# A streaming-encoder block on one core: weight sums of the second feed-forward made ahead and kept in DRAM, and more products by the seven-product form

## The chip, the core and the metric

The kernel runs on one core of one Trainium2 chip, in one launch. The metric is the time of an execution in microseconds (us); less is better. Engines are named as in the profile: PE (TensorE) multiplies matrices, DVE (VectorE) and ACT (ScalarE) work elementwise, POOL (GpSimd) here only issues some transfers and fills, SP (SyncE) issues nearly all transfers.

## What is computed

One layer over 256 tokens of 2048 features, in float32, cut to what matters here:

```python
def swiglu(h, w_up, w_down):
    gate, up = jnp.split(h @ w_up, 2, axis=-1)
    return (jax.nn.silu(gate) * up) @ w_down

x = x + 0.5 * swiglu(rms_norm(x, ffn1_norm), ffn1_w_up, ffn1_w_down)     # w_up 2048 x 11264, w_down 5632 x 2048
x = x + (sigmoid(gate_A) * hgrn2(h) + sigmoid(gate_B) * rglru(h)) @ w_out  # h = rms_norm(x) @ w_in, projected
x = x + cross_attention(rms_norm(x), rms_norm(mem))                       # 4 heads, 256 memory tokens
x = x + 0.5 * swiglu(rms_norm(x, ffn2_norm), ffn2_w_up, ffn2_w_down)
return rms_norm(x, final_norm)
```

The two feed-forwards are of one form. All that lies between them (projections, recurrences, branch merge, cross attention) is called the middle here.

## The kernel before

**Precision.** Each float32 operand is split into a high part `h` (rounded to the fp32r format by an ACT copy) and a low part `l = raw - h` (by DVE), as `split` does (L119 to L121). A product is then three matmuls: high by high, low operand by high weight, high operand by low weight (`three`, L448 to L454).

**Weights** come in pieces of 1 MB (128 partitions x 2048 float32), one after another in the order of `plan`. `weights()` (L165 to L182) hands a piece out and has the next one prepared ahead; `prepare` (L195 to L221) issues the load on SP's queue into `raw` (three buffers) and splits it into `h` (pool of three) and `l` (pool of three). A piece of kind "added" goes another way (`begin_added`, L186 to L193): a load into `own`, an ACT copy with scale -1 into `l`, and an accumulating transfer on POOL's queue that adds `own` to it, so that DVE has no part in it.

**A feed-forward** (`ffn`, from L467) walks 11 groups of 512 hidden columns. A group has eight up pieces; a piece p holds the four 128x512 blocks (two feature blocks, gate and up) of one pair of feature blocks. Then come two or four down pieces of earlier groups. The activation of a group goes through `ev`, is turned by transposes into `hidop`, and is used by the down pieces later. An up piece is multiplied in one of three forms (table `PRODUCTS`, L460 to L466), each product being three matmuls of 512 columns:

- "plain" (group 0): eight products;
- "mixed": eight products, with differences of the operand;
- "fast": seven products (24 matmuls become 21) out of sums and differences of the four operand blocks and of the four weight blocks, in the manner of Strassen and Winograd.

For a "fast" piece the sums of the weights are made each time: three DVE instructions (L213 to L215) write `td`, four blocks of 512 columns; `td` is then split into `th` (from the `h` pool) and `tl` in two halves. `td` and `tl` both come from the pool "wide", which has three buffers; `ev` and a scratch tile come from it too.

Before the change, both feed-forwards have the same list (`ffn_order`): groups 1 and 2 have four mixed and four fast pieces, groups 3 to 10 have two mixed (0 and 6) and six fast ones. The mixed ones from group 3, piece 6, on are "added".

**The order of the work.** The first pieces are ordered by hand; after that the order of instructions on each engine and on SP's queue is set when the program is built, and doesn't change while it runs. Matmuls of neighbouring pieces may stand interleaved. An engine and a queue work through their list in order, and an instruction whose operand or buffer isn't free holds up those behind it.

Of the kernel before, what the change touches and what calls it, by code (L numbers as in the profile page):

```python
# [13 lines left out]
P = 128  # L14
# [24 lines left out]
PAD = 16  # L39


def ffn_order():

    out, down = [("plain", 0, p) for p in range(8)], [("down", 0, 1, c, 0) for c in range(4)]
    for g in range(1, NG):
        if g < 3:  # L50
            out += [(("mixed", "fast")[p % 2], g, p) for p in (0, 1, 2, 3, 5, 4, 7, 6)]
# [10 lines left out]
def block_kernel(ctx: ExitStack, tc: tile.TileContext, xT, xin, memT, vec, gfin, bgate, lruw, wu1, wd1, win, wv,  # L62
# [55 lines left out]

    def split(h, l, raw):  # L119
        done["high"] = act.activation(h, raw, ACT.Copy).ins  # L120
        dve.tensor_tensor(out=l, in0=raw, in1=h.bitcast(F32), op=ALU.subtract)  # L121
# [6 lines left out]
    orders = dict.fromkeys(("ffn1", "ffn2"), ffn_order())  # L128

    def plan_ffn(name, wu, wd):  # L130
        for e in orders[name]:
            src = wd[e[4], e[3]] if e[0] == "down" else wu[e[1], e[2]]
            kind = "fast" if e[0] == "fast" else "added" if e[0] == "mixed" and e[1:] > (3, 0) else "plain"
            plan.append(((name,) + e, src, kind))

    def plan_columns(name, w, which):
# [3 lines left out]
        plan.extend(((name, g, kq), w[g, kq], "plain") for kq in range(w.shape[1]))  # L140

    plan_ffn("ffn1", wu1, wd1)
    for hf in range(2):
# [21 lines left out]
    def weights(*key):  # L165
        while plan and len(ahead) < 2:
            i = next(planned)
            k, src, kind = plan.pop(0)
            if i == 0:
                in_turn.enter_context(tc.manual_schedule(engines={sp.engine, act.engine, dve.engine}))  # L170
            if i < len(head):
                head[i]()
            if plan and plan[0][2] == "added":
                begun.append(begin_added(plan[0][1]))
            ahead.append((k, prepare(src, kind, 4 if i < 4 else 1)))
            if i in rest:
# [5 lines left out]
        return w  # L182

    begun = []

# [9 lines left out]
    def prepare(src, kind, cuts=1):  # L195
# [8 lines left out]
        if kind == "plain":  # L204
            h, l = split_tiles()
            for a in range(0, 2048, n):
                sp.dma_start(raw[:, a:a + n], src[:, a:a + n])
                split(h[:, a:a + n], l[:, a:a + n], raw[:, a:a + n])
            return h, l
        sp.dma_start(raw, src)  # L210
        td = scoped["wide"].tile([P, 2048], F32, name="td", tag="wide")
        two = [v[:, a:a + 1024].rearrange("p (i n) -> p i n", i=2) for v, a in ((td, 0), (raw, 512))]
        dve.tensor_tensor(out=two[0], in0=raw[:, None, :512].broadcast_to([P, 2, 512]), in1=two[1], op=ALU.subtract)  # L213
        dve.tensor_tensor(out=td[:, 1024:1536], in0=raw[:, 1024:1536], in1=td[:, :512], op=ALU.subtract)
# [122 lines left out]
            return r  # L337


    FFN_POOLS = dict(wide=3, own=1)  # L340

    class TokenSquares:

# [4 lines left out]
        def add(self, c, ts=range(2)):  # L348
            for t in ts:
                if "wide" in scoped:  # L350
                    junk = scoped["wide"].tile([P, 2048], F32, name="junk", tag="wide")[:, :512]
                else:
                    junk = scoped["tmp2"].tile([P, 512], F32, name="junk", tag="tmp2")
# [48 lines left out]

    BOTH = [2, 4]
    xd = []

    def operand_pairs(src, gain, q, xg, out):

        for a in src:  # L410
            i = len(out)
            g = xg[:, i * 512:(i + 1) * 512]
            for z in range(2):
                act.activation(g[:, z * T:][:, :T], a[:, z * T:(z + 1) * T], ACT.Copy,
                               scale=col(gain, 4 * q + 2 * i + z))
            h, l = slot(F32R, "xh"), slot(F32R, "xl")
            split(h[:, :512], l[:, :512], g)
            less = None if i else (h[:, 512:768], l[:, 512:768])
            if 2 * q + i in BOTH:
                if 2 * q + i == BOTH[0]:  # L420
                    xd.append(slot(F32R, "xd"))
                n = 512 * BOTH.index(2 * q + i)
                less = [xd[-1][:, a:a + 256] for a in (n, n + 256)]
            out.append(((h, l), less))

        def sums(which=((0, "less"), (0, "sums"), (1, "less"), (1, "sums"))):
            s = slot(name="xs")
            for i, ((h, l), less) in enumerate(out):
                a = [xg[:, i * 512 + j * P:][:, :P] for j in range(4)]

                def made(h, l, n, at, terms):
# [2 lines left out]
                        dve.tensor_tensor(out=o[j], in0=x, in1=y, op=op)  # L434
                    split(h, l, s[:, at:at + n * P])

                if less and (i, "less") in which:
                    made(*less, 2, 0, lambda o: ((a[0], a[1], ALU.subtract), (a[2], a[3], ALU.subtract)))
                if (i or 2 * q in BOTH) and (i, "sums") in which:
                    if not i and len(which) > 1:  # L440
# [26 lines left out]
    def ffn(name, pairs, sq, then, begin=(), sums=(), rstds=()):  # L467
# [39 lines left out]
        for at, e in enumerate(order):  # L507
# [3 lines left out]
            if kind != "down":  # L511
# [65 lines left out]
    def head_x(p):  # L577
# [7 lines left out]
        sums = operand_pairs([src[:, a:a + 512]], "ffn1_norm", q, xg, out)  # L585
        if p % 2:
            sums1.append(sums)
        pairs1.append(out[-1])
# [466 lines left out]

    def to_ffn(c):
        out = []
        sums2.append(operand_pairs(turned(xt[c]), "ffn2_norm", c, slot(name="xg"), out))
        pairs2.extend(out)
        if c < 2:  # L1060
            sums2.pop(0)()
# [130 lines left out]
```

## Time and profile before

| what | value |
|---|---|
| median of 3 runs | 2442.7 us (2442.57 to 2443.22) |
| the profiled execution's own time | 2442.24 us |
| its span, first to last instruction | 2440.5 us |
| PE, DVE, ACT busy, share of the span | 100%, 78%, 57% |
| HBM read, written | 472.07 MB, 2.10 MB |
| weights of the middle, first and last issue | 677.1 and 1709.4 us from the span's start |

Busy time is summed over an engine's instructions; matmuls overlap, so a matmul's own duration is longer than its share of the time. The granted clock (PEclk) is the share of full speed that TensorE was given. A DMA issue is counted from the issuing instruction to the landing of the last byte. In a row of a group of instructions stand: line, engine, operation, what is written and read, shapes and count; busy us and mean ns of one; and idle time of the engine before them, with what ended it.

### The profile page before, as it was taken

What the parts mean: (1) busy time and instruction counts of PE and PEld (TensorE: products, weight loads), DVE (VectorE), ACT (ScalarE), POOL (GpSimd) and SP (SyncE); (2) the same over time, 40 slices, a digit from 0 to 9 for tenths busy, and PEclk for the clock granted to TensorE, in tenths of its full rate; (3) what the DMA queues carried; (4) which work ended last, traced back from release to release, by engine and by line L of the source; (5) the groups of instructions that cost most, each with busy time, mean ns of one, the idle gap of its engine ahead of it and who ended that gap; (6) DMA issues with size and microseconds to landing.
All of it is one profiled execution on the core that took longest, in us unless ns stands there. A gap on an engine that the chain in (4) does not pass through costs nothing.

```text
span 2440.5 us, 30183 instructions
## 1 busy us (share of the span) xinstructions
PE 2430.0 (100%) x12250; PEld 2033.8 (83%) x12250; DVE 1892.8 (78%) x2016; ACT 1390.8 (57%) x1398; POOL 28.3 (1%) x36
## 2 busy tenths in 40 slices
PE   9999999999999999999999999999999999999998
PEld 8888888888888888888888888888888888888887
DVE  6999999999765757577565676556589999999995
ACT  8566666666554454477435554555555666666664
POOL 0000000000000000000000000000000000000000
PEclk9999999999999999999999999999999999999999
DMA  8557777677555545445555555544555677777763
GB/s 296 207 204 243 255 234 236 234 241 239 200 181 192 180 173 179 176 171 217 191 189 186 206 196 190 190 173 155 189 191 185 232 238 234 234 239 241 237 216 151
DMA packets 75020, 507.59 MB, mean 208 GB/s; under 512 B 8320, under 2 KB 8576, under 8 KB 15232
## 3 DMA queue, kind: packets, MB, share of 16 engines
q1 hardware_dynamic: 69840, 473.06, 53.3%
q0 software_dynamic: 4320, 31.46, 6.7%
q8 instruction: 96, 1.57, 0.2%
q10 hardware_dynamic: 720, 1.13, 0.1%
q14 instruction: 44, 0.36, 0.0%
HBM read 472.07 MB, written 2.10 MB: 194 GB/s over the span
## 4 chain that ended last, share of the span: by engine, by line
PE 97%; DVE 1%; ACT 1%; DMA 1%; issue 0%; SPq 0%; ACTq 0%; DVEq 0%
PE acc L451 18%; PE acc L454 18%; PE acc L452 18%; PE acc L231 11%; PE acc L252 8%; PE acc L253 8%; PE acc L255 8%; PE acc L235 6%; PE acc L491 1%; PE acc L391 1%; ACT h L120 0%; PE acc L768 0%; DVE l L121 0%; DMA xf<-xT 0%; PE acc L1051 0%; PE acc L1006 0%
## 5 line engine op out<-in xcount | busy, mean ns | idle before, releaser
L121 DVE TENSOR_TENSOR l<-raw,h 128x2048 fp32r<-128x2048 f32 (+2 forms) x422 | 877.9, 2087 | 364.8 <-ACT h L120 354.7
L120 ACT ACTIVATE h<-raw 128x2048 fp32r<-128x2048 f32 (+2 forms) x422 | 736.7, 1752 | 615.1 <-PE acc L253 206.2
L451 PE MATMUL acc<-h,xh 128*128 128x512 f32 x1280 | 499.0, 391 | 0.4 <-ACT h L120 0.3
L452 PE MATMUL acc<-h,xl 128*128 128x512 f32 x1280 | 496.9, 389 | 0.0
L120 ACT ACTIVATE h<-td 128x1024 fp32r<-128x1024 f32 x224 | 229.7, 1056 | 177.0 <-PE acc L452 130.8
L252 PE MATMUL acc<-h,ops 128*128 128x512 f32 x832 | 326.9, 393 | 0.0
L253 PE MATMUL acc<-h,ops 128*128 128x512 f32 x832 | 324.3, 390 | 0.0
L121 DVE TENSOR_TENSOR tl<-td,h 128x1024 fp32r<-128x1024 f32 x224 | 267.4, 1220 | 31.6 <-ACT h L120 29.0
L451 PEld LDWEIGHTS acc<-h,xh 128*128 128x128 f32 x1280 | 240.3, 188 | 53.2 <-ACT h L120 3.4
L452 PEld LDWEIGHTS acc<-h,xl 128*128 128x128 f32 x1280 | 240.3, 188 | 49.4
L231 PE MATMUL acc<-ops,h 128*128 128x512 f32 x1152 | 277.9, 393 | 0.2
L451 PE MATMUL acc<-h,hidop 128*128 128x512 f32 x704 | 275.7, 392 | 0.0
L452 PE MATMUL acc<-h,hidop 128*128 128x512 f32 x704 | 274.3, 390 | 0.0
L231 PEld LDWEIGHTS acc<-ops,h 128*128 128x128 f32 x1152 | 211.9, 188 | 42.8 <-DVE ops L292 0.9
L454 PE MATMUL acc<-l,xh 128*128 128x512 f32 x832 | 218.3, 389 | 0.0
L255 PE MATMUL acc<-l,ops 128*128 128x512 f32 x832 | 206.1, 390 | 0.0
L454 PE MATMUL acc<-l,hidop 128*128 128x512 f32 x704 | 188.3, 389 | 0.0
L255 PEld LDWEIGHTS acc<-l,ops 128*128 128x128 f32 x832 | 156.2, 188 | 32.4
L454 PEld LDWEIGHTS acc<-l,xh 128*128 128x128 f32 x832 | 156.0, 188 | 32.5
L252 PEld LDWEIGHTS acc<-h,ops 128*128 128x128 f32 x832 | 156.3, 188 | 32.3
L253 PEld LDWEIGHTS acc<-h,ops 128*128 128x128 f32 x832 | 156.3, 188 | 31.6
L454 PEld LDWEIGHTS acc<-l,hidop 128*128 128x128 f32 x704 | 132.2, 188 | 27.5
(220 smaller groups left out, 2347.9 us busy)
## 6 DMA issues: line engine op xcount, KB each, us to landing
raw<-wu SPq DMA_DIRECT2D x142, 1024.0 KB, 4.8
raw<-wd SPq DMA_DIRECT2D x88, 1024.0 KB, 4.8
raw<-win SPq DMA_DIRECT2D x40, 1024.0 KB, 4.8
raw<-wg SPq DMA_DIRECT2D x32, 1024.0 KB, 4.8
own<-wu SPq DMA_DIRECT2D x30, 1024.0 KB, 5.4
l<-own POOLq DMA_DIRECT2D x30, 1024.0 KB, 7.7
raw<-wab SPq DMA_DIRECT2D x16, 1024.0 KB, 4.8
raw<-wout SPq DMA_DIRECT2D x16, 1024.0 KB, 4.8
```

Of the source, the lines that this page charges most:

```text
L120: done["high"] = act.activation(h, raw, ACT.Copy).ins
L121: dve.tensor_tensor(out=l, in0=raw, in1=h.bitcast(F32), op=ALU.subtract)
L231: pe.matmul(acc, h[:, k * P:(k + 1) * P], xs[k], start=k == 0, stop=False)
L235: done["product"] = pe.matmul(acc[:, :T], l[:, k * P:(k + 1) * P], xs[k][:, :T], start=False, stop=k == KT - 1).ins
L252: pe.matmul(accs[t], x[:, t * P:][:, :P], h[j], start=first and j == 0, stop=False)
L253: pe.matmul(accs[t], x[:, T + t * P:][:, :P], h[j], start=False, stop=False)
L255: done["product"] = pe.matmul(accs[t], x[:, t * P:][:, :P], l[j], start=False, stop=last and j == 3).ins
L391: pe.transpose(accs[m // 2][:, m % 2 * T + t * P:][:, :P], tile[:, t * 512 + m * P:][:, :P], ident)
L451: pe.matmul(acc, ah, bh, start=start, stop=False)
L452: pe.matmul(acc, al, bh, start=False, stop=False)
L454: pe.matmul(acc, ah, bl, start=False, stop=stop)
L491: pe.transpose(acc[:, z * T + t * P:][:, :P], hid[t][:, (2 * y + z) * P:][:, :P], ident)
```

## The change

- **More fast pieces.** In the first feed-forward groups 3 to 10 have one mixed piece (6) in place of two. In the second, groups 1 and 2 have two mixed pieces (4 and 6) in place of four, and groups 3 to 10 have none. The order within groups 3 to 10 becomes 1, 3, 0, 6, 4, 2, 5, 7.
- **Sums made ahead.** For 52 of the second feed-forward's up pieces (list `MADE`: six in groups 1 and 2; pieces 0, 3, 4, 5 and 7 in groups 3 to 10) the sums of the weights are made during the middle: POOL's queue loads the piece into one buffer `made`, DVE makes four subtractions in place, POOL's queue stores the result to a tensor in DRAM. The 52 are spread over 170 pieces of the middle, and the subtractions stand two pieces behind their load.
- **Their use.** A made piece loads three quarters of its weights into `raw` and its sums, 1 MB, into `td`, both on SP's queue; `td` is split in one go.
- **Down pieces of the first feed-forward**: half of those of groups 1 to 8 become "added".
- **Buffers and operands.** The middle's pool `tmp` has six buffers in place of eight, `feature` two in place of three; a pool "third" is added for the feed-forwards. Which operand pairs get sums and which get differences follows from the new lists; three late sums of the first feed-forward are made at pieces 22, 23 and 24 in place of two at 17 and 18.

```diff
+MIXED = {
+    "ffn1": {1: (0, 2, 4, 6), 3: (6,)},
+    "ffn2": {1: (4, 6), 3: ()},
+}
+MADE = [(g, p) for g in range(1, NG) for p in range(8) if p not in ((4, 6) if g < 3 else (1, 6, 2))]
...
-            out += [("mixed" if p in (0, 6) else "fast", g, p) for p in (1, 3, 0, 4, 2, 6, 5, 7)]
+            out += [("mixed" if p in mixed[3] else "fast", g, p) for p in (1, 3, 0, 6, 4, 2, 5, 7)]
...
+    dram = pool("dram", 1, space=bass.MemoryType.DRAM)
...
-            kind = "fast" if e[0] == "fast" else "added" if e[0] == "mixed" and e[1:] > (3, 0) else "plain"
+            kind = "fast" if e[0] == "fast" else "plain"
+            if e[0] == "mixed" and e[1] > 2:
+                kind = "added"
+            if name == "ffn2" and e[0] == "fast" and e[1:] in MADE:
+                src, kind = (src, e[1:]), "made"
+            if name == "ffn1" and e[0] == "down" and 0 < e[1] < NG - 2 and (e[3] + e[4] - e[1]) % 2 == 0:
+                kind = "added"
...
+    between = between + 2, len(plan) - between - 6
...
+            make_ahead(i - between[0])
...
+    def make_ahead(i):
+
+        n, pieces = len(MADE), between[1]
+        if 0 <= i < pieces:
+            for j in range(i * n // pieces, (i + 1) * n // pieces):
+                makers.append((i + 2, make_sums(*MADE[j])))
+        while makers and (makers[0][0] == i or i == pieces):
+            makers.pop(0)[1]()
+
+    def make_sums(g, p):
+        raw = scoped["made"].tile([P, 2048], F32, name="made", tag="made")
+        r = [raw[:, i * 512:(i + 1) * 512] for i in range(4)]
+        nc.gpsimd.dma_start(raw, wu2[g, p])
+
+        def sums():
+            with tc.issue_after(done["low"]):
+                for o, a, b in ((1, 0, 1), (0, 0, 2), (2, 2, 1), (3, 3, 2)):
+                    dve.tensor_tensor(out=r[o], in0=r[a], in1=r[b], op=ALU.subtract)
+            kept = sums_kept[g, p] = dram.tile([P, 2048], F32, name=f"kept{g}_{p}", tag=f"kept{g}_{p}")
+            nc.gpsimd.dma_start(kept, raw)
+
+        return sums
...
+        td = scoped["wide"].tile([P, 2048], F32, name="td", tag="wide")
+        if kind == "made":
+            sp.dma_start(raw[:, 512:], src[0][:, 512:])
+            sp.dma_start(td, sums_kept[src[1]])
+            h, l = split_tiles()
+            split(h[:, 512:], l[:, 512:], raw[:, 512:])
+            th = hp.tile([P, 2048], F32R, name="h", tag="h")
+            tl = scoped["wide"].tile([P, 2048], F32R, name="tl", tag="wide")
+            split(th, tl, td)
+            return (h, l), (th, tl)
         sp.dma_start(raw, src)
-        td = scoped["wide"].tile([P, 2048], F32, name="td", tag="wide")
...
-    FFN_POOLS = dict(wide=3, own=1)
+    FFN_POOLS = dict(wide=3, own=1, third=1)
...
+                    if b in (4, 5) and fast and name == "ffn2" and (g, p) in MADE:
+                        b = 9 - b
...
-    for q, i in ((1, 17), (2, 18)):
+    for q, i in ((0, 22), (1, 23), (2, 24)):
         rest[i] = lambda q=q: sums1[q](((0, "sums"),))
...
-    middle.enter_context(scope(tmp=8, tmp2=2, scores=1, extra=2, feature=3))
+    middle.enter_context(scope(tmp=6, tmp2=2, scores=1, extra=2, feature=2, made=1))
```

More of the change, by code (lines that the diff above doesn't have):

```diff
@@ L50, in ffn_order @@
         if g < 3:
-            out += [(("mixed", "fast")[p % 2], g, p) for p in (0, 1, 2, 3, 5, 4, 7, 6)]
+            out += [("mixed" if p in mixed[1] else "fast", g, p) for p in (0, 1, 2, 3, 5, 4, 7, 6)]
         else:
-            out += [("mixed" if p in (0, 6) else "fast", g, p) for p in (1, 3, 0, 4, 2, 6, 5, 7)]
+            out += [("mixed" if p in mixed[3] else "fast", g, p) for p in (1, 3, 0, 6, 4, 2, 5, 7)]
         if g > 2 and g % 2:
@@ L142, in block_kernel @@
     plan_ffn("ffn1", wu1, wd1)
+    between = len(plan)
     for hf in range(2):
@@ L398, in normed, with operand_pairs @@
             ops.add(accs[m // 2][:, m % 2 * T:][:, :T], col(gain, 4 * c + m))
-    BOTH = [2, 4]
     xd = []
-    def operand_pairs(src, gain, q, xg, out):
+    def operand_pairs(name, src, gain, q, xg, out):
+        mixed = MIXED[name]
+        both = [p for p in mixed[1] if p not in mixed[3]]
         for a in src:
@@ L417, in operand_pairs @@
             split(h[:, :512], l[:, :512], g)
-            less = None if i else (h[:, 512:768], l[:, 512:768])
-            if 2 * q + i in BOTH:
-                if 2 * q + i == BOTH[0]:
+            less = None if 2 * q + i not in mixed[1] else (h[:, 512:768], l[:, 512:768])
+            if 2 * q + i in both:
+                if 2 * q + i == both[0]:
                     xd.append(slot(F32R, "xd"))
-                n = 512 * BOTH.index(2 * q + i)
-                less = [xd[-1][:, a:a + 256] for a in (n, n + 256)]
+                n = 512 * both.index(2 * q + i)
+                less = [xd[-1][:, a:a + 256] for a in (n, n + 256)] if n < 1024 else []
             out.append(((h, l), less))
@@ L435, in made @@
                     split(h, l, s[:, at:at + n * P])
+                if less == [] and (i, "less") in which:
+                    third = scoped["third"].tile([P, 512], F32R, name="xd", tag="xd")
+                    less.extend((third[:, :256], third[:, 256:]))
                 if less and (i, "less") in which:
                     made(*less, 2, 0, lambda o: ((a[0], a[1], ALU.subtract), (a[2], a[3], ALU.subtract)))
-                if (i or 2 * q in BOTH) and (i, "sums") in which:
-                    if not i and len(which) > 1:
+                if 2 * q + i not in mixed[3] and (i, "sums") in which:
+                    if not i and less and len(which) > 1:
                         s = slot(name="xs")
@@ L1057, in to_ffn @@
         out = []
[L1058 removed]
+        sums2.append(operand_pairs("ffn2", turned(xt[c]), "ffn2_norm", c, slot(name="xg"), out))
         pairs2.extend(out)
```

12 lines of the change are left out of this document (7 added, 5 removed).

## The prediction, made before the changed kernel had run

> **What bounds the kernel now.** First the page, then the busy time by stretches. Rows of the first fence: busy time of TensorE; granted clock; chain that ended last, by engine.
>
> ```profile
> PE 2430.0 (100%) x12250; PEld 2033.8 (83%) x12250; DVE 1892.8 (78%) x2016; ACT 1390.8 (57%) x1398; POOL 28.3 (1%) x36
> ...
> PEclk9999999999999999999999999999999999999999
> ...
> PE 97%; DVE 1%; ACT 1%; DMA 1%; issue 0%; SPq 0%; ACTq 0%; DVEq 0%
> ```
>
> TensorE is never out of work: a matmul less is time less, so long as its operands are there. The stretches (start:end, length, then busy us and instructions of PE, PEld, DVE, ACT, POOL, clock, DMA share, GB/s) are the middle with its seams and one group of the second feed-forward:
>
> ```profile
> 651.00:1790.00 1139.00, 1138.76 (x6474) 965.52 (x6473) 721.03 (x856) 598.34 (x701) 1.91 (x2) 1.00 0.52 184
> ...
> 1949.00:2011.00 62.00, 62.00 (x280) 51.40 (x279) 57.26 (x56) 38.34 (x32) 1.72 (x2) 1.00 0.73 238
> ```
>
> In the group DVE has 4.7 us to spare of 62, the DMA engines a quarter; the middle has slack in both. The pace, from the timeline of TensorE, where two "fast" pieces begin (21 matmuls each):
>
> ```profile
> 2082.35 0.39 PE L451 MATMUL acc<-h,xh 128*128 128x512 f32 x1
> ...
> 2087.11 0.39 PE L451 MATMUL acc<-h,xh 128*128 128x512 f32 x1
> ```
>
> 4.76 us for 21 matmuls is 0.227 us each; one ends 0.16 us after its slot, as it lasts 0.39.
>
> **What the change takes away.** Eight "mixed" pieces of the first feed-forward and 20 of the second become "fast": 28 products of three matmuls, 84 x 0.227 = **19.0 us**, 5.4 in the first and 13.6 in the second. TensorE's list in the changed program is indeed 84 matmuls shorter. If nothing ran late, 2442.7 - 19 = 2424.
>
> **What it puts on the path: second feed-forward.** The prices (first instructions grouped by form, the two ACT rows below; then DMA issues with the median us to landing; then, of a stretch with three loads 2.2 us apart, the issues and the landings):
>
> ```profile
> L121 DVE TENSOR_TENSOR l<-raw,h 128x2048 fp32r<-128x2048 f32 x294 | 671.4, 2289 | 341.1 <-ACT h L120 338.6 <-ACT lo L264 2.2
> L121 DVE TENSOR_TENSOR tl<-td,h 128x1024 fp32r<-128x1024 f32 x224 | 267.4, 1220 | 31.6 <-ACT h L120 29.0 <-PE acc L454 0.4
> L121 DVE TENSOR_TENSOR l<-raw,h 128x1536 fp32r<-128x1536 f32 x112 | 196.5, 1754 | 23.6 <-ACT h L120 16.1 <-PE acc L454 7.3
> L213 DVE TENSOR_TENSOR td<-raw 128x1024 f32<-128x1024 f32 x112 | 136.4, 1218 | 1.2 <-PE acc L454 1.0
> L215 DVE TENSOR_TENSOR td<-raw,td 128x512 f32<-128x512 f32 x112 | 77.2, 689 | 2.4
> L214 DVE TENSOR_TENSOR td<-raw,td 128x512 f32<-128x512 f32 x112 | 77.1, 688 | 2.0
> ```
>
> ```profile
> L120 ACT ACTIVATE h<-raw 128x2048 fp32r<-128x2048 f32 x294 | 561.0, 1914 | 455.4 <-PE acc L253 206.2 <-PE acc L452 105.2 <-PE acc L231 70.0
> L120 ACT ACTIVATE h<-td 128x1024 fp32r<-128x1024 f32 x224 | 229.7, 1056 | 177.0 <-PE acc L452 130.8 <-DVE td L213 20.4 <-DVE td L215 15.2
> ```
>
> ```profile
> raw<-wu SPq DMA_DIRECT2D x142, 1024.0 KB, 4.8
> ...
> l<-own POOLq DMA_DIRECT2D x30, 1024.0 KB, 7.7
> ```
>
> ```profile
> 86.89 0.33 SPq L207 DMA_DIRECT2D raw<-wd  x1
> 89.05 0.33 SPq L207 DMA_DIRECT2D raw<-wu  x1
> 91.25 0.33 SPq L210 DMA_DIRECT2D raw<-wu  x1
> ```
>
> ```profile
> DMA to landing us min/median/max: 4.7/5.6/6.5
> ```
>
> These three take 4.7, 5.6 and 6.5 us: a load waits for those issued ahead of it.
>
> Now the wait. Until now `td` is written by DVE from a `raw` that lies there already. After the change a made piece's `td` is the target of a load, and its slot in "wide" (three buffers, two per fast piece) comes free only when the product two pieces earlier has read its `tl` to the end. So load, ACT's split and DVE's split all begin after that. From that last slot: 0.16 + 4.8 landing + 1.91 = **6.9 us** to `th`, + 2.29 = **9.2** to `tl`. What TensorE has to do meanwhile is counted in its order in the changed program (groups 4 to 10 are alike; matmuls between the releasing one and the first on `th` / on `tl`):
>
> - piece 3: 51 / 62, that is 11.6 / 14.1 us. Hidden.
> - piece 0: 30 / 41, 6.8 / 9.3 us. Late by 0.1.
> - pieces 4 and 5: 27 / 38, 6.1 / 8.6 us. Late by 0.8 each.
> - piece 7: 21 / 29, 4.8 / 6.6 us. Late by 9.2 - 6.6 = 2.6 when its load is alone. It isn't: on SP's queue two loads of down weights stand just ahead of it. With the 6.5 us of the third in a row, `tl` is there at 10.9: late by **4.3**.
>
> DVE adds to it. The computed pieces 6 and 2 stand on DVE behind the `tl` of the made pieces 0 and 4, which wait for a landing: 2.29 + 1.22 + 1.75 + 0.69 + 1.22 + 0.69, then ACT 1.06, is 8.9 us (8.5 with the 0.07 by which DVE's instructions overlap in the timeline) from `th` of piece 0 to the second half of `th` of piece 6; TensorE has 33 matmuls, 7.5 us. Late by 1.0, in the same windows in which pieces 4 and 5 lack 0.8, so I count 1.0 for each pair, not 1.8.
>
> One group: 0.1 + 1.0 + 1.0 + 4.3 = **6.4 us** (4.3 with loads alone and the pairs at 0.8; 8.0 if two of the loads of pieces 0, 4 and 5 have one ahead, 0.8 later each), eight groups 51. Groups 1 and 2 have five made pieces in a row and then a sixth: 30 / 41 and 27 / 38 matmuls, 0.9 us with loads alone, but 1.75 MB a piece in 4.76 us fills the DMA engines, and each load then meets one ahead: I take 4 us a group (1 to 5), and 3 (0 to 4) for the first made piece of group 3, whose load follows those. Together **62 us late** (36 to 78), against 13.6 saved: **+48** (+22 to +64). DVE's sum is no gain here: a group has three computed pieces fewer (6.8 each) and five made ones more (1.75 + 2.29 each), within 0.2 us of before.
>
> By the Trainium skill ("DMA: Bandwidth & Descriptors", Anatomy of one DMA), a transfer takes about 2.0 us and its bytes at 436 GB/s, an estimate of 4.4 us for these loads; by it pieces 4, 5 and 7 would each be 0.4 earlier, some 10 us in all, and the sum 2489. The page's rule was fitted on another queue; the rows' 4.8 stands here.
>
> **First feed-forward.** Per group a fast piece more (1.75 + 1.22 + 0.69 + 0.69 + 2.44 = 6.8 us of DVE) and half of four down pieces through GpSimd's accumulating DMA (2 x 2.29 = 4.6 less): DVE goes from 57.3 of 62 to 59.5 of 60.7 us. It isn't the bound by its sum, but with 1.2 us to spare some of its waits reach TensorE: 0.7 us a group, 7 in all (0 to 15), against 5.4 saved: **+2** (-5 to +10).
>
> **Middle.** 52 pieces are loaded on GpSimd's queue, four subtractions of 128x512 each (52 x 4 x 0.69 = 143 us of DVE: 721 becomes 865 of 1139) and stored there. No work is taken from TensorE, so there is no gain. DVE has room; but it stands still while a made piece hasn't landed, with the next `l` behind it. One buffer makes a loop: 2.8 us of subtractions, store, load. A plain copy there isn't in the trace; it lies between the 4.8 and the 7.7 us above, nearer the first, since the second also reads its target: loop 12.4 to 18.2, taken 14, against 3.27 pieces. The weights of the stage's second half, first and last issue:
>
> ```profile
> L207 SPq DMA_DIRECT2D raw<-wab x16: 327/328/328, 1153.0 to 1236.6; - x16
> ...
> L207 SPq DMA_DIRECT2D raw<-wo x16: 327/328/328, 1612.6 to 1709.4; - x16
> ```
>
> 96 pieces in 556 us are 5.8 us each, 19 us a loop. Hidden mostly; where two waits meet, **+6** (0 to +30). Buffers fewer for `tmp` and `feature`: nothing, both are freed within a piece of 5.8 us. Operand sums: the second feed-forward makes two more (each four instructions of 128x128 and a split of 128x512, 0.69 the longest) and two differences fewer, ahead of its start, under DVE's slack of the middle; the first makes its three late ones at weights 22 to 24, before group 3 reads them; without that cover, some 2 us each.
>
> Sum: 48 + 2 + 6 = +56. The profiled execution took 2442.24 us (span 2440.5 and 1.7 around it), 0.5 under the median: **2499**.
>
> **Rivals.**
> - *The store loop binds the middle*: if a plain copy on GpSimd's queue takes the 7.7 us of the accumulating one and its 0.9 us of issue counts too, the loop is 2.8 + 2 x 8.6 = 20 us against 19: about 1 us for each of 29 loops, 2528. For it: landings in this queue are long; against: half the bytes. 0.12.
> - *Pauses slow the clock*: after a pause of 4 us the next matmuls may be granted less. No row shows it before the end, where TensorE has nothing to do; if as much time as the pause ran at half pace, 9 matmuls x 0.227 = 2 us for some 9 pauses, 2517. The Trainium skill ("TensorE: Matmul & The Clock Gate", What's actually happening) has the clock halved after an idle window of 3.4 us until a busy one; by it the estimate is 1.7 us a pause. The trace has no pause to test it. 0.06.
> - *The loads are in time* (faster): place, the freeing of "wide" before pieces 0, 4, 5 and 7; price, all of the 62 us. Piece 7 is late by the landing less 2.2, the pairs by 1.0 less what landing falls under 4.7; eight such groups eat the 19 us at a landing of 4.0 us. Below that the change gains, at the best 2424. For it: the shortest landing of a piece of weights is 3.7 us (row below); against: the median. 0.06.
>
> ```profile
> DMA to landing us min/median/max: 3.7/4.8/9.5
> ```
>
> **How the numbers follow.** Forecast 0.73, rivals 0.12, 0.06 and 0.06; 0.03 that lateness and saving cancel. A measurement of this kernel tells about 0.2% from no change. Faster 0.06, same 0.03, slower 0.91. Lower end: loads alone, +22 - 5 + 0 = 17, upper: +64 + 10 + 30 = 104. Not all meet: **2470 to 2540**, which takes in the first two rivals.
>
> **What would show it.** TensorE in the second feed-forward no longer 60 of 60 us; groups of 66 to 68 us in place of 62.1; the longest waits there for ACT's `h` from `td`, some 4 us once a group before the down pieces; landings of `td` of 5 to 7 us; about 84 matmuls fewer. Wrong it is if `td` lands in under 4 us, if the groups take 61 us, or if the middle has grown by over 30 us.

## The result, and the profile after

The changed kernel takes **2577.1 us** (median of 4 runs, 2575.3 to 2580.4) against 2442.7: a ratio of 1.055, 95% interval 1.0538 to 1.0568. It is slower, as forecast, but by 134 us and not by 56, and above the range. The profiled execution took 2577.73 us.

The three lines of the page that stood first for the kernel before (TensorE's busy time, the granted clock, the chain that ended last by engine):

```profile
PE 2472.5 (96%) x12166; PEld 2035.0 (79%) x12166; DVE 2012.9 (78%) x2171; ACT 1412.5 (55%) x1397; POOL 78.6 (3%) x134
...
PEclk9999999999999999999999999999999999999999
...
PE 66%; DMA 14%; DVE 10%; ACT 6%; issue 4%; SPq 0%; ACTq 0%; DVEq 0%; POOLq 0%
```

84 matmuls fewer, and TensorE is busy 42 us longer: busy time per matmul has grown. The clock's digits still say 9, but its mean over the execution is 0.98. DMA, DVE and ACT hold 30% of the chain, against 3% before. The same two stretches as before, by windows of the changed kernel (middle, one group), and a third behind one pause:

```profile
659.00:1838.00 1179.00, 1150.32 (x6476) 971.09 (x6475) 843.89 (x1064) 594.54 (x700) 56.87 (x105) 0.99 0.73 270
2179.00:2250.00 71.00, 65.44 (x275) 51.56 (x275) 56.98 (x47) 37.32 (x28) 0.00 (x0) 0.95 0.64 234
...
2212.00:2219.00 7.00, 6.08 (x17) 4.83 (x18) 6.09 (x3) 6.76 (x5) 0.00 (x0) 0.59 0.16 60
```

The stage borders are the first writes of `hidop` in a group, on ACT's timeline. The table has the span cut there.

| stage, us | before | after | difference |
|---|---|---|---|
| to the last `hidop` of the first feed-forward | 651.0 | 659.0 | +8.0 |
| from there to the first of the second (the middle, and group 0) | 1139.7 | 1179.1 | +39.4 |
| from there to the end of the span | 649.8 | 737.9 | +88.1 |
| one group of the second, from group 4 on | 62.1 (the last 61.1) | 69.2 to 72.0 | +7 to +11 |

**Where a group loses it.** One pause, in time order on SP's queue, ACT and PE:

```profile
2200.49 1.96 SPq L245 DMA_DIRECT2D raw<-wd  x2
2204.04 0.33 SPq L251 DMA_DIRECT2D td<-kept  x1
```

```profile
2210.96 1.91 ACT L124 ACTIVATE h<-td 128x2048 fp32r<-128x2048 f32 x1 [6.08 <-DMA td<-kept]
```

```profile
2207.93 0.84 PE L505 MATMUL acc<-l,xh 128*128 128x512 f32 x3
2212.93 0.80 PE L502 MATMUL acc<-h,xh 128*128 128x512 f32 x1 [4.15 <-ACT h L124]
```

Two loads of down weights, then piece 7's `td`, which takes 6.9 us until ACT reads it; TensorE stands 4.15 us. Then its first matmul lasts 0.80 us in place of 0.39: in the window 2212 to 2219 the granted clock is 0.59. In the trace's records of the clock it is half for 3.4 or 6.8 us at each such pause, from 2.1 to 4.1 us behind the pause's beginning on, so that a part of this time can fall into the pause itself. With 6.8 us in the first feed-forward and 3.4 to 10.2 us at some places of the middle it makes 96 us in all.

**Where the middle loses it.** Two rows of the waits (which engine waited for what: us in all, times, longest), and one round of the loop on POOL and DVE:

```profile
POOL made L211 <- DMA kept<-made: 258.2, 51, 9.2
...
DVE made L216 <- DMA made<-wu: 83.3, 22, 10.1
```

```profile
1198.35 0.54 POOL L218 DMA_DIRECT2D kept<-made  x1 [12.79 <-DVE made L216]
1206.65 0.53 POOL L211 DMA_DIRECT2D made<-wu  x1 [7.76 <-DMA kept<-made]
1220.50 0.55 POOL L218 DMA_DIRECT2D kept<-made  x1 [13.32 <-DVE made L216]
```

```profile
1215.15 0.69 DVE L216 TENSOR_TENSOR made<-made 128x512 f32<-128x512 f32 x1 [8.80 <-DMA made<-wu]
1217.96 2.13 DVE L216 TENSOR_TENSOR made<-made 128x512 f32<-128x512 f32 x3
```

Store 8.3 us, load 8.5, subtractions spread over 5 between the splits: a round of 22.2 us, where the pieces leave 19. DVE, which works in order, stands at the subtraction, and `l` for TensorE stands behind it. This round is longer than most. Worked out from the trace (store and load until they land, and the first to the last subtraction), the 51 rounds have a median of 15.6 us and go from 12.3 to 24.5; eight are over 19, and three of these lie between 1154 and 1245 us, around TensorE's longest pause of the middle (9.6 us).

### The profile page after: what moved, and what is told of

Same layout as the page of the kernel before. It is cut to its first block, busy times and chain, and to the rows that moved or that the text cites. A ratio compares the mean times of both kernels' runs of the same rounds, so it can differ in the third digit from the quotient of the medians.

```text
span 2576.0 us, 30541 instructions
## 1 busy us (share of the span) xinstructions
PE 2472.5 (96%) x12166; PEld 2035.0 (79%) x12166; DVE 2012.9 (78%) x2171; ACT 1412.5 (55%) x1397; POOL 78.6 (3%) x134
## 4 chain that ended last, share of the span: by engine, by line
PE 66%; DMA 14%; DVE 10%; ACT 6%; issue 4%; SPq 0%; ACTq 0%; DVEq 0%; POOLq 0%
PE acc L502 12%; PE acc L503 11%; PE acc L505 11%; PE acc L278 8%; DMA td<-kept 6%; PE acc L299 6%; PE acc L300 5%; PE acc L302 5%; ACT h L124 5%; PE acc L282 4%; DVE l L125 3%; DMA made<-wu 3%; DMA kept<-made 3%; DVE td L260 1%; DVE tl L125 1%
## 5 line engine op out<-in xcount | busy, mean ns | idle before, releaser
L502 PE MATMUL acc<-h,xh 128*128 128x512 f32 x1248 | 506.6, 407 | 61.1 <-ACT h L124 59.9
L124 ACT ACTIVATE h<-td 128x1024 fp32r<-128x1024 f32 (+1 forms) x228 | 284.0, 1252 | 344.2 <-DMA td<-kept 118.0
L125 DVE TENSOR_TENSOR tl<-td,h 128x1024 fp32r<-128x1024 f32 (+1 forms) x228 | 332.4, 1463 | 139.1 <-ACT h L124 138.7
L299 PE MATMUL acc<-h,ops 128*128 128x512 f32 x832 | 330.9, 398 | 3.1 <-ACT h L124 3.1
L300 PE MATMUL acc<-h,ops 128*128 128x512 f32 x832 | 327.9, 394 | 0.0
L216 DVE TENSOR_TENSOR made<-made 128x512 f32<-128x512 f32 x208 | 143.0, 687 | 86.4 <-DMA made<-wu 83.3
L505 PE MATMUL acc<-l,xh 128*128 128x512 f32 x688 | 187.3, 390 | 1.3 <-DVE l L125 1.3
L505 PE MATMUL acc<-tl,xh 128*128 128x512 f32 x560 | 164.1, 404 | 0.1
```

Source lines behind the costliest of these rows:

```text
L125: done["low"] = dve.tensor_tensor(out=l, in0=raw, in1=h.bitcast(F32), op=ALU.subtract).ins
L216: dve.tensor_tensor(out=r[o], in0=r[a], in1=r[b], op=ALU.subtract)
L299: pe.matmul(accs[t], x[:, t * P:][:, :P], h[j], start=first and j == 0, stop=False)
L300: pe.matmul(accs[t], x[:, T + t * P:][:, :P], h[j], start=False, stop=False)
L502: pe.matmul(acc, ah, bh, start=start, stop=False)
L505: pe.matmul(acc, ah, bl, start=False, stop=stop)
```

## The experiments

Each run has its own runs of the kernel before on its chip (2442.1 to 2442.3). Times are medians.

### One part at a time

**e1_first** keeps the first feed-forward's part alone, **e2_middle** makes and stores the sums without using them, **e3_use** has the second feed-forward's part alone: nothing is made ahead, and `td` is loaded from the weights, so that the output lacks the sums. The lists of mixed, fast and made pieces are put back where a part is left out.

```diff
-            make_ahead(i - between[0])                  # e1, e3
...
-            sp.dma_start(td, sums_kept[src[1]])         # e3
+            sp.dma_start(td, src[0])
```

> The first feed-forward's part alone (seven fast pieces of eight from group three on, half of its down pieces by the accumulating transfer); middle and second feed-forward as before. Theory: DVE is left about 1 us of slack a group there, and the lateness at the start of the added down pieces eats the 5.4 us saved: 2447 to 2453 us, 4 to 10 over before. Rival: the loss in the first feed-forward is small and the time goes elsewhere: 2437 to 2443.

> The middle's part alone: the 52 pieces' sums are made and stored with the smaller pools, and nobody reads them; both feed-forwards as before. Theory (the loop of load, subtractions and store through one buffer holds DVE up): 2475 to 2490 us, 32 to 47 over before, with DVE idle some 80 us before the subtractions. Rival (the middle's growth came from what the first feed-forward leaves behind): under 2455.

> The second feed-forward's part alone. It leaves out the making of the sums: the load into td takes the piece's weights themselves, of the same size and shape, so the output isn't the layer's. Theory (the load waits for its slot, and the pauses halve the clock): the second feed-forward still takes about 88 us more, 2520 to 2535 us in all, groups of 69 to 72 us. Rival (reading back what was stored in DRAM is what is slow): groups of 62 to 65, 2450 to 2480.

Measured: e1 **2449.7** (1.0020 to 1.0042), e2 **2476.4** (1.0123 to 1.0161), e3 **2530.8** (1.0344 to 1.0379). 7.7 + 34.3 + 88.7 = 130.7 of the 134: the parts add up, so each can be studied alone. e3's groups from four on take 71.0 to 72.3 us with nothing made in the middle; the loss there is in how the tiles are loaded, not in where they come from. All three came out within their theories.

In e1, groups 4 to 10 take 61.9 to 62.7 us, about as before: the 0.7 us saved there are given back, as the prediction had it. What takes them isn't shown; DVE is busy for 58.4 of 62 us there. Most of the rest is one place, group 3. The window of it in e1, the same group of before, and e1's wait in it:

```profile
163.00:222.00 59.00, 54.94 (x234) 43.48 (x233) 52.96 (x54) 37.85 (x31) 2.73 (x3) 0.97 0.75 234
```

```profile
163.00:217.00 54.00, 54.00 (x245) 44.22 (x244) 53.23 (x52) 35.97 (x29) 1.00 (x1) 1.00 0.67 233
```

```profile
204.08 0.76 PE L502 MATMUL acc<-l,hidop 128*128 128x512 f32 x2 [2.74 <-DMA l<-own]
```

The first "added" down piece is not there: 2.7 us, a half clock of 3.4 us behind it, and 5 us in the group.

### The second feed-forward: the slot, the queue, the clock

**e4_wide4**: the whole change with four "wide" buffers in the second feed-forward.

```diff
-    with scope(**FFN_POOLS):
+    with scope(wide=4, third=1):
```

> The whole change, but in the second feed-forward the pool wide has four buffers (the unused buffer own gives the room), so that a td no longer waits for the product two pieces earlier. Theory (the slot's release starts the late loads): groups of 60.8 to 64 us in place of 70.7, no pause over 3 us, clock back at 1.00 there, 2480 to 2505 us in all. Rival (DVE's and the DMA engines' throughput is the bound, not the slot): groups of 67 or more, over 2545.

Measured: **2559.6** (1.0464 to 1.05). The theory missed by 55 us, and the rival's time came out. The pauses before piece 7 are all there, of 3.7 to 5.1 us, though a fourth buffer is there for its tile. SP's queue and ACT in e4:

```profile
2182.38 1.96 SPq L245 DMA_DIRECT2D raw<-wd  x2
2185.15 0.33 SPq L251 DMA_DIRECT2D td<-kept  x1
```

```profile
2192.36 1.91 ACT L124 ACTIVATE h<-td 128x2048 fp32r<-128x2048 f32 x1 [5.76 <-DMA td<-kept]
```

`td` is still issued behind two loads of down weights, and ACT reads it 7.2 us later. One more slot alone does not help here; the place in the queue is the cause left to test. The rival's reason, that DVE or the DMA engines are the bound, is refuted by e10 below.

**e5_inplace** splits a made tile in place, so that it takes one wide buffer; that also puts the `td` of piece 7 ahead of the down loads. **e10_in4** adds the fourth buffer, **e11_in4td** turns round the two loads of a made piece.

```diff
-            tl = scoped["wide"].tile([P, 2048], F32R, name="tl", tag="wide")
+            tl = td.bitcast(F32R)
```

> The whole change, with one difference in the second feed-forward: a made piece's split is written in place over its loaded tile, so that it takes one wide buffer and not two, and the loads of pieces 5 and 7 stand together in SP's queue ahead of the down loads. Theory (a load that is issued late and stands behind two down loads starves TensorE once a group, and the clock is halved after it): the pauses of over 3 us before piece 7 go, the granted clock in the second feed-forward is 1.00, groups from four on take 61 to 64 us, and the whole 2490 to 2505. Rival (VectorE or the DMA engines cannot deliver a group's weights faster than some 70 us): groups stay at 68 or more, the whole 2545 or more.

> e5_inplace with four wide buffers in place of three and no own buffer in the second feed-forward, where nothing is prepared by the added kind. Theory (what is left of e5's pauses, 2.1 to 3.6 us once a group, is still td loads issued late for a slot): groups from four on 61 to 63 us, the whole 2485 to 2500. Rival (the raw slots, of which there are three, or the transfers, hold SP's queue): groups as in e5, the whole 2510 to 2520.

> e10_in4 with the two loads of a made piece in the other order on SP's queue: the sums' tile first, which needs a wide slot, then the raw tile, which needs a raw slot. If the raw slots hold SP's queue and with it the sums' loads (rival of e10), this is faster than e10 by 5 to 15 us; if the wide slots were all, it equals e10 within 5 us; if the raw tile is what TensorE needs first, it is slower by 5 us or more.

Measured: e5 **2517.9** (1.0296 to 1.033), e10 **2475.4** (1.0115 to 1.0152), e11 **2472.3** (1.0108 to 1.0151; e10 and e11 can't be told apart). e5's groups take 63.7 to 67.9 us, between its theory and its rival: pauses of 1.6 to 3.2 us are left. As in-place splitting frees a slot and moves the load at once, e5 doesn't tell the two apart. With both edits the pauses go. e10 came out 10 us under its theory's range, and e11, equal to it, says that the order of the two loads doesn't matter there. SP's queue and one group of e10:

```profile
2072.71 5.56 SPq L251 DMA_DIRECT2D td<-kept  x2
2078.36 12.44 SPq L245 DMA_DIRECT2D raw<-wd  x4
```

```profile
2047.00:2108.00 61.00, 61.00 (x274) 50.35 (x273) 56.76 (x48) 37.39 (x29) 0.00 (x0) 1.00 0.72 272
```

61.0 us a group, 1.1 under before: TensorE is never out of work, at a DMA share of 0.72 and 272 GB/s. So neither DVE nor the DMA engines set the 71 us; late issues did, with what they cost in clock. From the first `hidop` to the end e10 takes 638.3 us against 649.8: the second feed-forward's saving, forecast as 13.6 us, is there as 11.5.

**e8_fill**: the whole change, with 14 matmuls by a tile of zeros, which add nothing, where TensorE pauses for piece 7.

```diff
+            if fill and i == 3:
+                for _ in range(fill):
+                    pe.matmul(acc, zero, products[0][2][0], start=False, stop=False)
```

> The whole change, with 14 matmuls by a tile of zeros (they add nothing) placed ahead of the first use of piece 7's weights in the second feed-forward's groups from the fourth on, where TensorE pauses for 4 to 5 us. The weights arrive no sooner; TensorE is only kept busy in the pause. Theory (the pause of over 3 us halves the clock for 3.4 us or more behind it, so that a late load is paid one and a half times or more): the half-clock intervals behind these pauses go, some 3 us for each of 7 or 8 groups, 2550 to 2557. Rival (the clock after a pause costs nothing that the next wait would not have taken anyway): 2573 to 2582 or more.

Measured: **2566.3** (1.0483 to 1.0527), 10.8 us less than the change by medians, between the two expectations. In the profiled executions, first the change, then e8, the clock of the same stretch:

```profile
1979.00:2500.00 521.00, 475.10 (x1981) 373.79 (x1980) 417.00 (x341) 277.04 (x208) 0.00 (x0) 0.96 0.64 235
```

```profile
1975.00:2500.00 525.00, 505.34 (x2188) 399.42 (x2187) 433.46 (x358) 286.34 (x215) 0.00 (x0) 1.00 0.67 242
```

No half clock is left in this stretch, and groups 3 to 10 take 544.1 us against 562.3: by the profiles 2.3 us a group of the loss was the clock, with weights that come no sooner. By the medians it is 10.8 us, 1.4 a group; e8's profiled execution was its fastest. The direction is shown; the size only as far as these two figures agree.

### The middle: what the loop costs

**e6_nostore** is e2 without the stores; **e7_halves** is e2 with the buffer cut into two halves that go round on their own (the pool `made` has two of them).

```diff
-            nc.gpsimd.dma_start(kept, raw)               # e6
...
-        raw = scoped["made"].tile([P, 2048], F32, name="made", tag="made")
+        for c in range(2):                               # e7
+            raw = scoped["made"].tile([P, 1024], F32, name="made", tag="made")
```

> The sums are made in the middle as in e2_middle, but not stored to DRAM and not used (left out: the stores, and the use in the second feed-forward). Theory (the one buffer goes round load, subtract, store, and the store is a third of the loop, so the middle's subtractions bunch up): most of e2_middle's 34 us goes, the whole 2455 or less. Rival (the added work of VectorE, the added loads or the smaller pools cost the time): 2465 or more.

> As e2_middle (sums made and stored, not used), but the one buffer of the sums is cut into two of half the size, which go round on their own: while one is stored the other is loaded or subtracted into. The work is the same. Theory (one buffer): 2445 to 2462. Rival (work of VectorE, DMA traffic or smaller pools): 2470 or more.

Measured: e6 **2448.2** (1.0016 to 1.0034), e7 **2704.1** (1.1061 to 1.1094). e6 does DVE's 143 us of subtractions and the loads, with the smaller pools, and loses 6 us: of e2's 34 us, 28 belong to the store. e7 went far the wrong way. POOL's queue in e7, and DVE's wait for the loads there:

```profile
1305.37 0.79 POOL L212 DMA_DIRECT2D made<-wu  x1 [4.74 <-issue]
1312.92 0.76 POOL L212 DMA_DIRECT2D made<-wu  x1 [6.76 <-DMA made<-wu]
1319.07 0.74 POOL L220 DMA_DIRECT2D kept<-made  x1 [5.40 <-DVE made L219]
1322.70 0.72 POOL L220 DMA_DIRECT2D kept<-made  x1 [2.88 <-issue]
1326.75 0.79 POOL L212 DMA_DIRECT2D made<-wu  x1 [3.33 <-issue]
```

```profile
DVE made L219 <- DMA made<-wu: 380.3, 83, 12.1
```

The halves hardly overlap: POOL issues the second load 7.5 us after the first. A round is still 21.4 us, and DVE can stand twice in it. Half a piece, taken in rows of 1 KB, lands in a median of 5.3 us against 6.3 for a whole one in the change, so that four transfers cost more than two. Why the second load waits for the first's landing stays open; two halves on one queue are no remedy here, which says nothing against two whole buffers: these weren't tried.

**e9_pool** has GpSimd make the sums of e2, **e14_pool2** the same with a clearing moved from GpSimd to VectorE, **e16_pool40** the same in a whole version with 40 pieces, whose first feed-forward is that of before and whose second has e11's buffers.

```diff
-                    dve.tensor_tensor(out=r[o], in0=r[a], in1=r[b], op=ALU.subtract)
+                nc.gpsimd.tensor_tensor(out=r[o], in0=r[a], in1=r[b], op=ALU.subtract)
...
-        nc.gpsimd.memset(S[:, :1024], 0.0)               # e14, e16
+        dve.memset(S[:, :1024], 0.0)
```

> As e2_middle (sums made and stored, not used), with one difference: the four subtractions of a piece are done by GpSimd, which also issues the load and the store, and not by VectorE. Load, subtract, store then go round on GpSimd's queue alone, and a late load holds back nothing in VectorE's order. Theory (the store makes the next load late, and VectorE, which works in order, stands at that piece's subtractions while TensorE's own splits wait behind it): the middle falls to within 10 us of the 1140 us of before, the whole 2444 to 2455. Rival (the traffic of 104 more transfers slows the loads that TensorE waits for): the middle stays at 1165 or more, the whole 2467 or more.

> e9_pool (GpSimd makes the sums) with the clearing of one tile of the memory stage, which stood 75 us behind sums in GpSimd's order there, done by VectorE. Theory (that wait was e9's loss beyond e2's): the 75 us pause goes and with it its half clock, the middle 1145 to 1185, the whole 2450 to 2490. Rival (GpSimd's subtractions themselves hold VectorE or the loads back): 2520 or more.

> As e15_dve40, but GpSimd makes the sums, in all stages of the middle, 40 pieces at some 23.6 us against e14's own round of 20 to 23 us, so that it need not lag, and the tile's clearing is VectorE's. Theory (e9's and e14's long pauses came from the lag of GpSimd's loop behind its places in the order): no pause over 10 us, the middle 1140 to 1165, the whole 2435 to 2460. Rival (GpSimd's subtractions hold VectorE back wherever they run): 2465 or more.

Measured: e9 **2566.0** (1.0478 to 1.0551), e14 **2555.8** (1.0438 to 1.0488), e16 **2455.5** (1.004 to 1.0067). e9 and e14 missed their theories (2444 to 2455, 2450 to 2490), e16 met its own. e9 and e14 each have one long pause of TensorE, 75 and 91 us. Their waits at that place:

```profile
ACT S L855 <- POOL S L824: 84.1, 1, 84.1
...
PE acc L296 <- ACT h L124: 74.6, 1, 74.6
```

```profile
ACT h L124 <- DMA raw<-wvm: 103.0, 1, 103.0
```

In e9 ACT waits for a clearing that GpSimd has behind its sums; in e14, where VectorE does the clearing, this wait is gone. But there the next weights are late. GpSimd's last store in e14, then SP's queue:

```profile
1667.87 0.58 POOL L215 DMA_DIRECT2D kept<-made  x1 [0.41 <-POOL made L213]
```

```profile
1672.19 0.33 SPq L225 DMA_DIRECT2D own<-wu  x1
1672.62 23.48 SPq L242 DMA_DIRECT2D raw<-wvm  x6
```

SP's queue issues nothing for 110 us before, and goes on 4.3 us after the last store with the second feed-forward's first load into `own`, which the kernel before issues at 1542; the six loads of `wvm` stand behind it. That `own` waited for the buffer of the sums, and so for the end of GpSimd's loop (20.5 us a round in the median), is argued, not shown. With 40 pieces (e16) no pause is over 5.7 us. But e16 makes fewer sums and also has no load into `own` in its second feed-forward, so it leaves open which of the two took the long pause away; it does show that sums on GpSimd need not cost one.

### A version that pays

**e12_skip46**, **e13_skip52**, **e15_dve40**, **e18_mix3** and **e19_mix3_42** put it together: first feed-forward as before, second as e11, subtractions on VectorE, and no sum begun in plan slots 62 to 92 (gate and ab stages, where e2's waits were longest; a plan slot is one of the middle's 170 pieces). They differ in how many pieces are made; e18 and e19 also have three mixed pieces in groups 1 and 2.

```diff
+        slots = [s for s in range(between[1]) if not 62 <= s < 93]
...
+            if slots[j * pieces // n] == i:
                 makers.append((i + 2, make_sums(*MADE[j])))
...
+    "ffn2": {1: (2, 4, 6), 3: ()},                       # e18, e19
```

> A version put together from what the runs say: the first feed-forward as before; the second as in e11_in4td; in the middle no sum is begun in the 31 plan slots (62 to 92) of the gate and ab stages, where VectorE stood at subtractions whose load had not landed, and 46 pieces in place of 52 (three, not six, in groups one and two), so that the loop keeps some 17 us a round elsewhere. Theory (e2's loss sits in those stages alone): first 651, middle 1140 to 1152, second 637 to 641 with the ends, 2430 to 2446 in all. Rival (a round of the loop that is too short anywhere gives the loss back, or the stores cost wherever they are): 2455 or more.

> As e12_skip46 with all 52 pieces, so that the loop has some 15 us a round outside the two stages, where e2's shortest rounds were 14 to 16 us. Theory (the round of load, subtract and store against the spacing of the pieces sets the loss): 10 us or more above e12, 2445 to 2475. Rival (only the two stages matter): within 5 us of e12.

> As e12_skip46 with 40 pieces (groups from three on; in groups one and two the fast pieces' sums are made on VectorE in place), so that a round of the loop has 19 us outside the two stages. Theory (round against spacing): the middle's loss falls from 16.5 us to 4 to 9 us, groups one and two take 52 to 56 us, the whole 2438 to 2450. Rival (the middle's loss is the same for any round above the loop's own): the whole 2452 or more.

> As e15_dve40, with three and not two pieces of groups one and two by eight products (pieces 2, 4 and 6), so that VectorE makes the sums of five pieces there and not of six. In e15 these two groups took 53.9 and 56.1 us, with pauses at the sums' tile, against 51.4 and 51.8 in e12. If VectorE is what they waited for, they take 51.5 to 53 us and the whole 2436 to 2440, faster than before by 0.1 to 0.25%; if the added matmuls take that back, 2441 to 2444.

> As e18_mix3, with piece 5 of groups one and two made ahead too: 42 pieces, 3.3 plan slots a round in place of 3.5. If the loop's round has slack at 3.5 slots (e15's middle lost 2.4 us), the middle loses 4 to 8 us and the groups gain 0 to 2: 2438 to 2446. If only the loop's traffic counts, within 2 us of e18.

| kernel | plan slots a round | DVE stands for loads, us | middle, us over before | time, us | interval of the ratio |
|---|---|---|---|---|---|
| e13, 52 pieces | 2.7 | 172.4 | 81.0 | 2516.4 | 1.0289 to 1.0321 |
| e12, 46 | 3.0 | 60.9 | 16.5 | 2455.1 | 1.0037 to 1.0063 |
| e2, 52, no slots skipped | 3.3 | 77.3 | 32.7 | 2476.4 | 1.0123 to 1.0161 |
| e19, 42 | 3.3 | 22.2 | 6.5 | 2439.3 | 0.9976 to 0.9994 |
| e15, 40 | 3.5 | 18.0 | 2.4 | 2442.7 | 0.9994 to 1.0012 |
| e18, 40 | 3.5 | 18.0 | 2.8 | **2436.0** | **0.9968 to 0.9986** |

The times are medians; the columns before them are of the profiled execution, which was the fastest in e12 and e13. The middle's loss goes with the round that the pieces leave, and with the time for which DVE stands. e2 and e19 leave the same round; e19, which skips the two stages and makes ten pieces fewer, loses 26 us less. Rows of the waits in e13, e12 and e18:

```profile
DVE made L217 <- DMA made<-wu: 172.4, 42, 10.8
```

```profile
DVE made L217 <- DMA made<-wu: 60.9, 20, 11.0
```

```profile
DVE made L217 <- DMA made<-wu: 18.0, 5, 5.9
```

DVE stands 42 times in e13, 20 in e12 and 5 in e18. e13's 2.7 slots are, at 5.8 us a piece, an estimate of 15.5 us, no more than the median round of 15.6 in the changed kernel, so that most rounds are late; it came out 41 us above its theory's range, though on the side of e12 that it forecast. e12 stayed 9 us above its theory: six pieces fewer were not enough, and its rival's mechanism, a round too short anywhere, is the table's. e15 is right: the middle all but free. Its groups 1 and 2 take 53.9 and 56.1 us; with five computed pieces there in place of six (e18) 51.8 and 51.6. e18 and e19 are within their theories. **e18 is faster than both kernels**, than the one before by little: 6.2 us by medians, the interval clear of 1. Its page and a late group:

```profile
PE 2420.6 (99%) x12196; PEld 2023.2 (83%) x12196; DVE 1995.6 (82%) x2128; ACT 1384.6 (57%) x1380; POOL 58.0 (2%) x101
...
PE 96%; DVE 2%; ACT 1%; DMA 1%; issue 0%; SPq 0%; DVEq 0%; ACTq 0%
```

```profile
2010.00:2071.00 61.00, 61.00 (x275) 50.31 (x274) 57.15 (x48) 37.57 (x28) 0.00 (x0) 1.00 0.72 272
```

## Why the prediction was right and where it was wrong

- **84 matmuls, 19 us**: right. The count is 12250 less 12166, and where nothing is late (e10) the second feed-forward gains 11.5 of its 13.6 us.
- **Piece 7 late by 4.3 us, behind two down loads**: right in place and size; the pauses there are 3.4 to 5.0 us, 4.3 in the mean. e4, e5 and e10 show that a free slot and an earlier issue were both needed.
- **Groups of 66 to 68 us, +48 in all**: this failed, +88. Against e10's 61.0, groups 4 to 10 are late by 9.8 us each and not by 6.4. Worked out from the trace, the 9.8 are 5.7 of pauses, 2.2 of half clock while TensorE works, and 1.9 that stand in no pause and stay open. So the step that failed there is that a late load was paid by its pause alone. The other failing term is groups 1 to 3: I took 4, 4 and, with 3 for its first made piece, 9.4 us; against e10 (51.3, 51.3, 50.9) they lose 9.7, 5.9 and 15.8. The reason given, that these loads fill the DMA engines, fails: e10 carries the same loads without a pause, at a DMA share of 0.83 in group 1. Late issues behind a pause are the likely cause, not a shown one.
- **The rival of the clock**, given 0.06: it held. I priced it at 2 us a pause, which e8 (1.4 to 2.3) and the records of the clock (2.2) bear out, but set it beside the forecast as an unlikely case instead of adding it, though the forecast itself had a pause of 4.3 us in every group. The Trainium skill ("TensorE: Matmul & The Clock Gate", What's actually happening) has the clock halved after an idle window of about 3.4 us; by that rule a group pays an estimated 1.7 us. The records here agree with the 3.4 us as the step of the half clock, not as the least pause that brings it (2.7 us in e1 did); in groups 4 to 10, counted while TensorE works, they are worth 1.4 to 3.1 us.
- **Middle, +6 (0 to +30)**: failed, +34 alone (e2) and +39 in the whole, a growth that the prediction itself named as a sign of being wrong. The mechanism, DVE standing at a piece that hasn't landed, was the prediction's; the step that failed is one round, "taken 14", for a loop whose rounds differ. Load and store measured 6.3 and 4.5 us by their medians, and the median round, 15.6, is near the 14. But load and store take over 8 us each in the long rounds, the subtractions are spread in DVE's order, not 2.8 us together, and eight of 51 rounds pass the 19 us that the pieces leave. The rival of the store loop named the cause and, at 0.12, was held too unlikely; its price, 1 us lost in each of 29 rounds, is near the 34 by luck, as the loss sits in a few rounds. e6, e12, e13 and e15 settle that the loop's round is the cause.
- **First feed-forward, +2 (-5 to +10)**: 7.7 alone, inside its range. The 0.7 us a group was about right in size; the first added down piece in group 3 was not foreseen. One sum is wrong: a group less one fast piece's saving is 62.1 - 0.7 = 61.4 us and not 60.7, so DVE had 1.9 us to spare by it and not 1.2; the 0.7 us was taken and not worked out from it.
- **No gain by DVE's sum**: right, 57.0 of 71 us in a group against 57.3 of 62.
- **The range** took the bounds of each term, then left their upper ends out as "not all meet". All of them together make +104, still under the +134: the second feed-forward and the middle each went past its own upper end, 88 against 64 and 34 to 39 against 30.

## What to carry to other kernels

A tile that is loaded in place of computed takes on the queue's order and its buffer's release: check for each whether its load is issued a landing before its first use, with what stands ahead of it in the queue, and give it one buffer more before judging the idea. A side job of load, compute and store on one buffer needs spacing above its long rounds and not only above the median, including what its own compute waits for in an engine's order; under that, the loss climbs steeply (2.4, 16.5 and 81 us for 40, 46 and 52 pieces). Where a forecast contains pauses of TensorE of some microseconds, the half clock behind them belongs to the sum.

## What the runs showed of the hardware

Subtractions on GpSimd and on VectorE slow each other. Rows of GpSimd in e9 where VectorE stands still, and where it works; then a split on VectorE beside them:

```profile
1030.37 5.28 POOL L213 TENSOR_TENSOR made<-made 128x512 f32<-128x512 f32 x4 [4.46 <-DMA made<-wu]
...
1349.15 9.47 POOL L213 TENSOR_TENSOR made<-made 128x512 f32<-128x512 f32 x4 [5.72 <-DMA made<-wu]
```

```profile
1331.68 3.13 DVE L125 TENSOR_TENSOR l<-raw,h 128x2048 fp32r<-128x2048 f32 x1 [2.31 <-ACT h L124]
```

Four take 5.28 us alone (so do five in a row in e14's long pause) and 9.47 beside VectorE, against 2.87 for four on VectorE; VectorE's split of 2.29 us takes 3.13. Spans on GpSimd are rough in these profiles. The Trainium skill ("SBUF — State Buffer", Who interferes with whom) has the two share a pair of ports as an exclusive lock, and a VectorE instruction with two inputs in SBUF contend there with a GpSimd instruction that reads SBUF; these rows agree with that, as both get slower. That the ports are the cause is not shown by a run.

The half clock comes in steps of 3.41 us: of 121 intervals in these traces (the one at each execution's end left out) 60 last one step, 41 two, 18 three to six (10.2 to 20.5 us), and the two at the long pauses of e9 and e14 last 22 and 29 steps (75 and 99 us). Each pause of TensorE of over 3.2 us was followed by one, which began in the pause or up to 1.5 us behind it; only two pauses of 5.2 us, in e9 and e14, brought none, as they lie inside one that ran already. Of pauses of 2 to 3.2 us only some were: 2.7 us in e1 had one, and 3.06 us had one in the changed kernel and none, at the same place, in e6.
